# A hybrid decoder layer on one core: an order of emission written with other clock estimates, and a lead of its own for two steps

## The chip, the cores and the metric

The kernel runs on one core of a Trainium2 chip. Its time is the device time of one execution in microseconds (us), and lower is better. The span of a profile is the time from the first to the last instruction that the profiler saw.

The engines go by the profile's names: PE multiplies matrices (PEld loads its weights), ACT applies functions and copies, DVE and POOL work elementwise, SP issues the transfers (DMA). Each engine runs its own queue strictly in the order in which the program emitted it. An instruction that waits for data holds back everything behind it on that engine.

## What is computed

The reference is one decoder layer. A normalised input h (2048 tokens by 1024) is multiplied by a wide matrix w_in; one part of the result feeds a gated delta rule with 8 heads in chunks, the other a short gated convolution; both meet in a second product with w_out.

```python
h = rmsnorm(x, norm_in_w)
proj = h @ w_in
qkv, z_g, b_g, a_g, gate_b, gate_c, h_c, z_c = jnp.split(proj, split_at, axis=-1)
qkv = jax.nn.silu(causal_depthwise_conv(qkv, conv_qkv_w))
...
o = gated_delta_rule_chunked(q, k, v, g, beta)
o = rmsnorm(o, gdn_norm_w) * jax.nn.silu(z_g)
y_c = gate_b * (causal_depthwise_conv(gate_c * h_c, conv_w) + conv_b)
y_c = y_c * jax.nn.silu(z_c)
return rmsnorm(x + jnp.concatenate([o, y_c], -1) @ w_out, final_norm_w)
```

## The kernel before

**The products.** The tokens are taken in two halves of 1024. The columns of w_in are taken in 32 pairs of 128 columns, numbered 0 to 31 here, and each half has one "quad" per pair: seven block products, each of 4 x 3 matmuls of 128x512 in f16 that write the tile ps_d, so 84 matmuls for a quad. They are called large products here. The gates add 40 more behind the quad of pair 0. Counting the large products in PE's queue, the quad of pair p (p from 1 on) begins after 84 p + 40 of them. After both halves come 1536 large products with w_out.

**The preparation of a pair.** In the first half the weights of each pair are made on the way. `fetcher` has SP load two tiles `raw` of 512 KB (four such buffers in all, so a pair's loads wait until an earlier pair is done with). `scales` squares both tiles on ACT, with the sums of the rows in the tile `wss` (written as junk_sq,wss<-raw); one small matmul on PE with a matrix of ones, ps_t<-wss,ones_b, sums them over the partitions. It is called the column sum here. DVE and POOL make a scale `wsc` of it (the tile p on the way); ACT and DVE then write the high and the low f16 part of each weight block (g<-raw), and PE's products read g. SP stores g to DRAM (wc), and the second half only loads it again (gr).

**The order.** The program that emits the instructions keeps a clock of its own for each engine (`Clock`): `cost` is what an instruction is thought to take, `emit` books it and says when its result is thought to be there, transfers included. Steps are generators. `do` emits an instruction once its inputs are thought to be ready by the present time of PE plus a lead (`LEAD`: -0.4 us for PE, 0 for ACT, DVE and POOL, -2.0 for SP); until then other steps and the large products go first. `either` chooses between POOL and DVE for some elementwise steps by the two clocks. At the end `keep_order` fixes each engine's queue in just this order, so these clocks say nothing of how long anything takes on the chip, but they decide what stands behind what.

**The other work.** For each head and half `gdn` prepares the chunks and runs the recurrence (matmuls to ps_r and ps_o, and elementwise steps on DVE and ACT between them); `invert` works through a triangular inverse on POOL (nb, nbt) and goes through DRAM (nd, wd) on the way in and out; `gdn_post` ends a half head (its matmul with `fold` reads the tile op). `later_x` brings in the second half's tokens.

Of the kernel before, what the change touches and what calls it, by code (L numbers as in the profile page):

```python
# [12 lines left out]
BF16 = mybir.dt.bfloat16  # L13
I32 = mybir.dt.int32
AF = mybir.ActivationFunctionType
# [6 lines left out]
DRAM = bass.MemoryType.DRAM  # L22
BACK = 1.2
DRAIN, SEM = 0.2, 0.06
LEAD = {"PE": -0.4, "ACT": 0.0, "DVE": 0.0, "POOL": 0.0, "SP": -2.0}
ORDER = ("PE", "ACT", "DVE", "POOL", "SP")


def is_ap(x):
    return hasattr(x, "tensor") and hasattr(x, "ap")  # L30


class Clock:
# [11 lines left out]
    def box(self, ap):  # L45
        ten = ap.tensor
        name = ten.name
        row = self.rows.get(name)
        if row is None:
            row = 0  # L50
            if ap.space != DRAM:
                row = 1
                for n in list(ten.shape)[1:]:
                    row *= n
            self.rows[name] = row
        pat = list(ap.ap)
        off = ap.offset
        if row:
            p0, f0 = divmod(off, row)
            p1 = p0 + pat[0][1]  # L60
            pat = pat[1:]
        else:
            p0, p1, f0 = 0, 1, off
        f1 = f0 + 1
        for step, n in pat:
            f1 += abs(step) * (n - 1)
        return name, p0, p1, f0, f1

    @staticmethod
    def latest(entries, b, eng):  # L70
# [34 lines left out]
    def cost(self, eng, op, outs, ins, a, k):  # L105
        o = outs[0]
        n = 1
        for s in list(o.shape)[1:]:
            n *= s
        ps = any(x.space == PSUM for x in ins) or o.space == PSUM  # L110
        if eng == "PE":
            if op == "transpose":
                return max(0.06, 0.11 * n / 128)
            lhs = a[1]
            if lhs.dtype == F32:
                return max(0.066, 4 * n / 2370 + 0.006)
            if lhs.dtype == F32R:
                return n / 2370 + 0.013
            return n / 2370
        if eng == "ACT":  # L120
            func = a[2] if len(a) > 2 else k.get("func")
            d = (n + (205 if ps else 246)) / 1200
            if is_ap(k.get("scale")) or is_ap(k.get("bias")):
                d += 0.09
            if "accum_out" in k:
                d += 0.2
            if func in (AF.Exp, AF.Silu):
                if self.func != func:
                    d += 1.29
                self.func = func  # L130
            return d
        if eng == "DVE":
            if op == "tensor_reduce":
                n = 1
                for s in list(ins[0].shape)[1:]:
                    n *= s
            if op in ("tensor_scalar", "tensor_copy", "memset") and not ps:
                return (n / 2 + 110) / 960 + 0.06
            d = (n + 150) / 960 + (0.06 if op == "scalar_tensor_tensor" else 0.0)
            return d if ps or n < 256 else 1.08 * d  # L140
        if eng == "POOL":
            if k.get("op") == ALU.pow:
                return 0.55 + 0.185 * n
            if op == "tensor_tensor":
                return 0.4 + min(0.0028 * n, 0.1 + 0.002 * n)
            return 0.2 + 0.0011 * n
        return 0.4

    def emit(self, eng, op, a, k):
        self.n += 1  # L150
        outs, ins = self.parts(a, k)
        start = max(self.t[eng], self.ready(eng, a, k))
        d = self.cost(eng, op, outs, ins, a, k)
        who = eng
        if eng == "SP":
            who = "DMA"
            self.t[eng] = start + d
            n = 1
            for s in list(outs[0].shape):
                n *= s  # L160
            size = 2 if outs[0].dtype in (F16, BF16) else 4
            self.dma = max(self.dma, start + 1.2) + n * size / 190e3 + 0.1
            done = max(self.dma, start + 1.5 + n * size / 110e3) + 0.8
            free = done
        else:
            self.t[eng] = free = start + d
            done = free + (DRAIN if eng == "PE" else SEM)
        now = self.t["PE"]
        for store, aps, t in ((self.wr, outs, done), (self.rd, ins, free)):
            for ap in aps:  # L170
                b = self.box(ap)
                old = [e for e in store.get(b[0], ()) if e[4] > now - 1.0]
                old.append((b[1], b[2], b[3], b[4], t, who))
                store[b[0]] = old
                if self.last.get(b[0], 0.0) < t:
                    self.last[b[0]] = t
# [36 lines left out]
def hybrid_layer_kernel(ctx, tc, x, norm_in_w, w_in, conv_qkv_w, A_log, dt_bias, gdn_norm_w,  # L213
# [3 lines left out]
    PE, ACT, DVE, POOL, SP = (Engine(clk, r, k) for r, k in zip(  # L217
        (nc.tensor, nc.scalar, nc.vector, nc.gpsimd, nc.sync), ORDER))
# [46 lines left out]
    def const(shape, name, dt=F32):  # L265
        return const_.tile(shape, dt, tag=name, name=name)

    tasks, done = [], set()
    marks, seq = [0], [0]

    def now():
        return clk.t["PE"]
# [6 lines left out]
    def mark(*key):  # L279
        done.add(key)  # L280
        marks[0] += 1
# [35 lines left out]
    def need(*keys):  # L317
        while not all(k in done for k in keys):
            yield None
# [4 lines left out]
    def do(fn, *a, back=BACK, lead=None, **k):  # L324
        e = fn.eng
        lead = LEAD[e] if lead is None else lead
        while True:
            t = clk.ready(e, a, k)
            cur, q = now(), clk.t[e]
            late = t > (cur if lead < 0 else max(cur, q)) + lead  # L330
            if not late and q <= cur + back:
                break
            yield max(t - max(lead, 0.0) if late else 0.0, q - back, cur + 0.1)
        fn(*a, **k)
# [12 lines left out]
    def acq(kind):  # L347
        while not slots[kind]:
            yield None
        return bank(kind)  # L350
# [5 lines left out]
    def rel(x, n=1):  # L356
        if isinstance(x, str):
            cred[x] += n
        else:
            name = x.tensor.name  # L360
            kind, tag = where.pop(name)
            where[tag] = clk.last.get(name, 0.0)
            slots[kind].append(tag)
        marks[0] += 1
# [47 lines left out]
    for half in range(2):  # L412
        convs = [(f, half, g) for g in range(G) for f in ("ca", "cb")]
        for i in range(H):
# [3 lines left out]
            n = ((4, 2, 2, 2, 2, 2, 1, 1), (2, 1, 2, 1, 2, 1, 2, 2))[half][i]  # L418
# [42 lines left out]
    ones_b = const([P, P], "ones_b", BF16)  # L461
# [26 lines left out]
    def pow2_below(o, sq, gain):  # L488
        n = sq.shape[-1]
        r = sm.tile([P, 2], F32, tag="p2", name="p2")[:, 0:n]  # L490
        yield from do(DVE.tensor_scalar, r, sq, 1e-30, None, op0=ALU.max)
        yield from do(POOL.tensor_tensor, r, r, nhalf_pow[:, 0:n], op=ALU.pow)
        yield from do(DVE.tensor_tensor, r.bitcast(I32), r.bitcast(I32), expo[:, 0:n].bitcast(I32),
                      op=ALU.bitwise_and)
        yield from do(DVE.tensor_scalar, o, r, gain, None, op0=ALU.mult)
# [199 lines left out]
    def scales():  # L695
        for p in range(NP):
            yield from need(("raw", p))
            s2, inv1, rho = (wsc[:, p, j:j + 1] for j in (1, 2, 4))
            ss = sm.tile([P, 2], F32, tag="wss", name="wss")
            for j in range(2):  # L700
                yield from do(ACT.activation, junk_sq, raws[p, j].rearrange("p k c -> p (k c)"),
                              AF.Square, accum_out=ss[:, j:j + 1])
            pt = yield from acq("t")
            yield from do(PE.matmul, pt[:, 0:2], ones_b, ss.bitcast(BF16)[:, 1::2], start=True, stop=True)
            yield from pow2_below(wsc[:, p, 0:2], pt[:, 0:2], 8192.0)
            rel(pt)
            yield from do(DVE.reciprocal, wsc[:, p, 2:4], wsc[:, p, 0:2])
            yield from do(DVE.tensor_scalar, rho, s2, inv1, None, op0=ALU.mult)
            yield from do(DVE.tensor_scalar, wsc[:, p, 2:4], wsc[:, p, 2:4], isx, None, op0=ALU.mult)
            mark("s", p)  # L710
# [787 lines left out]
    spawn(fetcher(), 0)  # L1498
    first_x()
    spawn(scales(), 0)  # L1500
    spawn(prepare_hi(), 1)
    spawn(prepare_lo(), 1)
# [105 lines left out]
```

## Time and profile before

| | |
|---|---|
| time, median of 3 runs | 2168.21 us (2161.38 to 2171.83) |
| the profiled execution's own time | 2169.81 us |
| its span | 2168.1 us |
| mean granted TensorE clock | 0.945 |
| busy: PE, DVE, POOL, ACT | 1940.2, 1391.7, 977.0, 968.1 us |
| moved by DMA | 302.66 MB, 139 GB/s over the span |

The table says that PE is the busiest engine, with 228 us of the span in which it runs nothing. To see where, one reads the 40 slices of the page first (each 54 us wide), then the busy time by stretches, and in a stretch with gaps the list of instructions in order of time with the idle time before each and what ended it. The granted clock has two levels, 1.0 (2.4 GHz) and 0.5 (1.2 GHz); a mean between them tells how much of a stretch ran at either.

### The profile page before, as it was taken

How to read it: one execution, taken by the hardware profiler on the slowest of the kernel's cores; microseconds unless marked ns; L12 is line 12 of the kernel's file. 1: busy time of each engine (PE TensorE's matmuls, PEld its weight loads, DVE VectorE, ACT ScalarE, POOL GpSimd, SP SyncE). 2: the span in 40 equal slices, each digit the busy share in tenths (PEclk: the TensorE clock that was granted, in tenths of full speed). 3: DMA queues.
4: the chain of work that ended last, by engine and by line, in shares of the span. 5: the costliest groups of instructions: out<-in, count | busy, mean ns of one | idle time of the engine just before them, and what ended most of it. 6: DMA issues, size and time to landing. Idle time of an engine off the chain costs nothing.

```text
span 2168.1 us, 29898 instructions
## 1 busy us (share of the span) xinstructions
PE 1940.2 (89%) x10832; PEld 1058.4 (49%) x10832; DVE 1391.7 (64%) x2547; ACT 968.1 (45%) x1889; POOL 977.0 (45%) x1228
## 2 busy tenths in 40 slices
PE   3699885889687979898999999999999999999998
PEld 2244342435444545454455655555655655444443
DVE  5689865886677877886466667766767644433221
ACT  6465555455353554644254444453543423333210
POOL 2226721286556736475366538467457451100000
PEclk9899987999798989998999999999999999999999
DMA  6348666355474765557354445545543447343210
GB/s 172 82 106 200 164 172 162 102 134 148 69 145 69 174 120 147 121 140 265 108 170 153 156 130 185 187 141 187 179 123 112 127 130 296 112 141 107 69 49 29
DMA packets 231194, 302.66 MB, mean 140 GB/s; under 512 B 48381, under 2 KB 161414, under 8 KB 230150
## 3 DMA queue, kind: packets, MB, share of 16 engines
q1 hardware_dynamic: 231046, 300.75, 50.3%
q8 instruction: 85, 1.39, 0.3%
q14 instruction: 63, 0.52, 0.1%
HBM read 188.36 MB, written 112.33 MB: 139 GB/s over the span
## 4 chain that ended last, share of the span: by engine, by line
PE 53%; DVE 2%; issue 1%; ACT 1%; DMA 1%; POOL 0%; DVEq 0%; POOLq 0%; SPq 0%; ACTq 0%
PE ps_d L188 44%; PE ps_t L188 5%; PE ps_r L188 3%; PE ps_o L188 2%; DVE kq L188 1%; DMA raw<-in_w_in_dram 1%; DVE c L188 0%; ACT c L188 0%; ACT junk_sq L188 0%; ACT L188 0%; DVE vacc L188 0%; DVE p L188 0%; DVE zb L188 0%; ACT sq L188 0%; DVE wq L188 0%
## 5 line engine op out<-in xcount | busy, mean ns | idle before, releaser
L188 PE MATMUL ps_d<-xop,g 128*128 128x512 f16 x2688 | 660.9, 397 | 37.2 <-ACT xop L188 12.8
L188 PE MATMUL ps_d<-xop,gr 128*128 128x512 f16 x2688 | 651.1, 382 | 0.0
L188 PEld LDWEIGHTS <-g 128*128 128x128 f16 x2688 | 269.1, 102 | 383.7 <-issue 115.0
L188 POOL TENSOR_TENSOR nbt<-nb 32x30 f32<-32x30 f32 (+14 forms) x480 | 320.7, 668 | 148.6 <-DMA nb<-nd 114.1
L188 PEld LDWEIGHTS <-gr 128*128 128x128 f16 x2688 | 261.8, 99 | 242.2 <-issue 6.3
L188 ACT ACTIVATE c<-ps_d 128x512 f32<-128x512 f32 x320 | 189.9, 594 | 374.4 <-PE ps_d L188 365.9
L188 POOL TENSOR_TENSOR nb<-nb,nbt 32x30 f32<-32x30 f32 (+14 forms) x480 | 323.7, 674 | 35.5
L188 PE MATMUL ps_d<-wo,mm 128*128 128x512 f16 x1536 | 336.7, 381 | 3.2 <-ACT mm L188 3.2
L188 PEld LDWEIGHTS <-mm 128*128 128x128 f16 x1536 | 149.7, 98 | 184.8 <-ACT mm L188 5.1
L188 POOL TENSOR_TENSOR oss<-oss,nhalf_pow 128x16 f32<-128x16 f32 x32 | 96.1, 3002 | 166.5 <-DVE oss L188 148.3
L188 DVE SCALAR_TENSOR_TENSOR kq<-c,wq,kq 128x512 f32<-128x512 f32 x192 | 164.4, 862 | 8.1 <-ACT kq L188 3.9
L188 POOL TENSOR_TENSOR p<-p,nhalf_pow 128x2 f32<-128x2 f32 (+1 forms) x51 | 40.2, 788 | 283.3 <-DVE p L188 275.2
L188 DVE SCALAR_TENSOR_TENSOR res<-ps_d,msc,res 128x512 f32<-128x512 f32 x32 | 22.6, 747 | 193.8 <-PE ps_d L188 193.8
L188 DVE SCALAR_TENSOR_TENSOR g<-raw,wsc,g 128x1024 f16<-128x1024 f32 (+1 forms) x96 | 114.2, 1194 | 8.9 <-ACT g L188 8.5
L188 ACT ACTIVATE g<-raw,wsc 128x1024 f16<-128x1024 f32 (+1 forms) x96 | 95.7, 1002 | 50.3 <-PE ps_d L188 32.1
L188 DVE TENSOR_TENSOR c<-ps_d,c 128x512 f32<-128x512 f32 x128 | 87.5, 684 | 44.5 <-PE ps_d L188 44.0
L188 ACT ACTIVATE junk_sq<-raw 128x1024 bf16<-128x1024 f32 x64 | 67.5, 1055 | 96.0 <-DMA raw<-in_w_in_dram 95.0
L188 POOL TENSOR_TENSOR stat<-stat,nhalf_pow 128x1 f32<-128x1 f32 x16 | 9.1, 570 | 217.7 <-DVE stat L188 216.8
L188 DVE TENSOR_TENSOR c<-c,c 128x1024 f32<-128x1024 f32 (+1 forms) x70 | 71.3, 1019 | 46.6 <-ACT c L188 43.9
L188 ACT ACTIVATE mm<-mr,msc 128x1024 f16<-128x1024 f32 x32 | 36.0, 1148 | 138.6 <-PE ps_d L188 111.6
L188 POOL TENSOR_TENSOR c<-c,c 128x512 f32<-128x512 f32 (+1 forms) x26 | 42.7, 1642 | 121.3 <-ACT c L188 87.9
L188 ACT ACTIVATE u<-ps_r 128x128 f32<-128x128 f32 x128 | 35.1, 274 | 124.7 <-PE ps_r L188 124.0
(226 smaller groups left out, 2793.1 us busy)
## 6 DMA issues: line engine op xcount, KB each, us to landing
gr<-wc SPq DMA_DIRECT2D x96, 512.0 KB, 3.8
raw<-in_w_in_dram SPq DMA_DIRECT2D x64, 512.0 KB, 10.3
wc<-g SPq DMA_DIRECT2D x64, 512.0 KB, 8.6
wc<-g SPq DMA_DIRECT2D x96, 256.0 KB, 2.7
wor<-in_w_out_dram SPq DMA_DIRECT2D x32, 512.0 KB, 5.4
mr<-mixd SPq DMA_DIRECT2D x32, 512.0 KB, 5.3
x<-in_x_dram SPq DMA_DIRECT2D x16, 512.0 KB, 6.7
E<-gd SPq DMA_DIRECT2D x16, 512.0 KB, 5.4
```

The source lines that it names most:

```text
L188: return raw(*a, **k)
```

## The change

Three things change, all of them in the program that emits.

The clock prices a transfer otherwise. Before, all transfers shared 190 KB per us with 0.1 us each, began 1.2 us after the issue and counted as landed 0.8 us after their end, with 110 KB per us as the most for a single one. Now the rate depends on the shorter contiguous run of the two sides (330 KB per us x run / (run + 700), run in bytes, by the new function `run_of`), the start is 1.5 us after the issue and the landing 2.5 us after the end. A tile of `raw` has runs of 512 bytes.

POOL's two-operand steps are priced at 0.3 us + 0.0023 us per element, where it was 0.4 us + the lesser of 0.0028 and 0.1 + 0.002 per element.

The squares of a pair from 1 on get a lead of -4.0 us (`SAFE`), and their column sum one of -3.0 us, in place of 0 and -0.4.

```diff
+SAFE = -4.0
...
+    def run_of(ap):
+        run, rest = 1, list(ap.ap)
+        if ap.space != DRAM:
+            rest = rest[1:]
+        for step, n in reversed(rest):
+            if step == run:
+                run *= n
+            elif n > 1:
+                break
+        return run
...
             if op == "tensor_tensor":
-                return 0.4 + min(0.0028 * n, 0.1 + 0.002 * n)
+                return 0.3 + 0.0023 * n
...
-            self.dma = max(self.dma, start + 1.2) + n * size / 190e3 + 0.1
-            done = max(self.dma, start + 1.5 + n * size / 110e3) + 0.8
+            run = min(self.run_of(outs[0]), self.run_of(ins[0])) * size
+            self.dma = max(self.dma, start + 1.5) + n * size / (330e3 * run / (run + 700)) + 0.1
+            done = self.dma + 2.5
...
                 yield from do(ACT.activation, junk_sq, raws[p, j].rearrange("p k c -> p (k c)"),
-                              AF.Square, accum_out=ss[:, j:j + 1])
+                              AF.Square, accum_out=ss[:, j:j + 1], lead=SAFE if p else None)
             pt = yield from acq("t")
-            yield from do(PE.matmul, pt[:, 0:2], ones_b, ss.bitcast(BF16)[:, 1::2], start=True, stop=True)
+            yield from do(PE.matmul, pt[:, 0:2], ones_b, ss.bitcast(BF16)[:, 1::2], start=True, stop=True,
+                          lead=-3.0 if p else None)
```

Every engine's queue comes out in another order, from the first 100 us to the last head. Three places follow, each before and then changed. Numbers behind names only tell one buffer from another; they differ between the two programs.

The first is PE's queue at the column sum of pair 13. Before, it stands behind the same large product as pair 12's (the first row), ahead of the quad of pair 11:

```order
L188 MATMUL ps_t_2882<-wss_2764,ones_b_168 128x2
L188 MATMUL ps_t_2920<-ident_161,x2_620 128x128 x2
L188 MATMUL ps_t_2920<-ident_161,x2_621 128x128 x2
L188 MATMUL ps_t_2938<-ident_161,x2_620 128x128 x2
L188 MATMUL ps_t_2938<-ident_161,x2_621 128x128 x2
L188 LDWEIGHTS ones_b_168
L188 MATMUL ps_t_2949<-wss_2915,ones_b_168 128x2
L188 MATMUL ps_r_2983<-S_all_214,kq_849 128x128
L188 MATMUL ps_o_2982<-kq_849,S_all_214 128x128
L188 MATMUL ps_r_2983<-r_2984,Wt0_215 128x128
L188 MATMUL ps_t_2995<-ident_161,kq_2966 128x128
```

Changed (the first row is a large product of the quad of pair 11):

```order
L202 MATMUL ps_d_3119<-xop_226,g_2916 128x512
L202 MATMUL ps_t_3180<-kq_2979 128x256 x2
L202 LDWEIGHTS ones_b_168
L202 MATMUL ps_t_3154<-wss_2974,ones_b_168 128x2
L202 MATMUL ps_r_3139<-u_3191,kst_1250 128x128
L202 MATMUL ps_o_2963<-NA_1296,u_3191 128x128
L202 LDWEIGHTS g_2916
```

It stood behind 964 large products and stands behind 1033, inside the quad of pair 11 instead of ahead of it.

The second is ACT's queue at the squares of pair 19 (kss are sums for the keys of a head, c1 and c2 results of the quads, u and oc belong to the recurrence). Before:

```order
L188 ACTIVATE kq_4378<-c2_3728,wq_3889 128x4x128
L188 ACTIVATE c2_4169<-c2_4169,wsc_123 128x1024
L188 ACTIVATE u_4446<-ps_r_4419 128x128
L188 ACTIVATE junk_sq_156,wss_4430<-raw_4404 128x1024
L188 ACTIVATE junk_sq_156,wss_4430<-raw_4363 128x1024
L188 ACTIVATE junk_4464,kss_4381<-ps_t_4423 128x128
```

Changed:

```order
L202 ACTIVATE junk_4629,kss_4290<-ps_t_4571 128x128
L202 ACTIVATE c2_4552<-ps_d_4616 128x512
L202 ACTIVATE junk_sq_156,wss_4525<-raw_4510 128x1024
L202 ACTIVATE junk_sq_156,wss_4525<-raw_4474 128x1024
L202 ACTIVATE oc_4671<-ps_o_4301 128x512
L202 ACTIVATE g_4660<-st_4489,wsc_123 128x512
```

The sums for the keys, which stood behind the squares, stand ahead of them now, and so does a result of the quad. PE's column sum of this pair went from behind 1468 large products to behind 1536.

The third is PE's queue where the quad of pair 8 begins. Before (g_2141 is the first weight block of pair 8; the column sum of that pair stands 28 large products ahead of it, outside this piece):

```order
L188 LDWEIGHTS g_2059
L188 MATMUL ps_d_1996<-xop_224,g_2059 128x512
L188 LDWEIGHTS g_2141
L188 MATMUL ps_d_2191<-xop_221,g_2141 128x512
L188 LDWEIGHTS g_2141
```

Changed (g_2351 is that block there):

```order
L202 MATMUL ps_r_2314<-S_all_214,kq_732 128x128
L202 LDWEIGHTS ones_b_168
L202 MATMUL ps_t_2276<-wss_2000,ones_b_168 128x2
L202 LDWEIGHTS g_2196
L202 MATMUL ps_d_2044<-xop_224,g_2196 128x512
L202 LDWEIGHTS g_2196
L202 MATMUL ps_d_2044<-xop_224,g_2196 128x512
L202 MATMUL ps_o_2219<-kq_732,S_all_214 128x128
L202 MATMUL ps_r_2314<-r_2315,Wt0_215 128x128
L202 MATMUL ps_r_2314<-u_2335,kst_1124 128x128
L202 MATMUL ps_o_2219<-NA_1184,u_2335 128x128
L202 MATMUL ps_r_2344<-S_all_214,kq_732 128x128
```

Between this column sum and the quad that needs it stand two large products and a step of the recurrence now.

Over all 32 pairs the column sum stands later in 28, by 3 to 96 large products, at the same place in 2 and earlier in 2. `either` sends ten steps to POOL that went to DVE.

## Rows read from the trace of the kernel before

**Rows 1.** The page: busy time by engine; the 40 slices of PE and its clock.

```profile
PE 1940.2 (89%) x10832; PEld 1058.4 (49%) x10832; DVE 1391.7 (64%) x2547; ACT 968.1 (45%) x1889; POOL 977.0 (45%) x1228
PE   3699885889687979898999999999999999999998
PEclk9899987999798989998999999999999999999999
```

**Rows 2.** Busy time by stretches: span, length, engines (instructions), PE clock, DMA share, GB/s.

```profile
100.00:1050.00 950.00, 793.76 (x4328) 432.06 (x4327) 712.36 (x1268) 494.32 (x941) 499.12 (x577) 0.90 0.59 143
400.00:1000.00 600.00, 508.03 (x2847) 283.37 (x2846) 468.11 (x800) 302.90 (x577) 371.19 (x444) 0.90 0.57 130
1050.00:1800.00 750.00, 743.27 (x4648) 436.70 (x4647) 497.49 (x906) 319.06 (x680) 421.25 (x573) 0.99 0.48 150
1800.00:2168.00 368.00, 352.60 (x1652) 163.35 (x1650) 115.93 (x243) 96.55 (x168) 26.28 (x34) 0.99 0.33 113
```

**Rows 3.** The tile wss: its matmuls, and PE's idle us before them (times).

```profile
L188 PE MATMUL ps_t<-wss,ones_b x32: 163/163/167, 29.7 to 957.5; 128*128 128x2 bf16 x32
...
  ACT junk_sq L188: 74.3, 17
```

**Rows 4.** PE in order of time: start, us, instruction, idle before it and its end.

```profile
360.65 0.16 PE L188 MATMUL ps_t<-wss,ones_b 128*128 128x2 bf16 x1 [1.16 <-ACT junk_sq L188]
...
373.57 0.16 PE L188 MATMUL ps_t<-wss,ones_b 128*128 128x2 bf16 x1 [11.51 <-ACT junk_sq L188]
...
569.03 0.16 PE L188 MATMUL ps_t<-wss,ones_b 128*128 128x2 bf16 x1 [10.94 <-ACT junk_sq L188]
...
624.39 0.16 PE L188 MATMUL ps_t<-wss,ones_b 128*128 128x2 bf16 x1 [9.59 <-ACT junk_sq L188]
...
688.76 0.16 PE L188 MATMUL ps_t<-wss,ones_b 128*128 128x2 bf16 x1 [8.93 <-ACT junk_sq L188]
...
780.84 0.16 PE L188 MATMUL ps_t<-wss,ones_b 128*128 128x2 bf16 x1 [7.53 <-ACT junk_sq L188]
```

**Rows 5.** The wait of 10.94 us: second load's issue, ACT's square, five us within.

```profile
547.91 0.38 SPq L188 DMA_DIRECT2D raw<-in_w_in_dram  x1
...
566.64 1.06 ACT L188 ACTIVATE junk_sq<-raw 128x1024 bf16<-128x1024 f32 x1 [13.23 <-DMA raw<-in_w_in_dram]
...
560.00:565.00 5.00, 0.00 (x0) 0.00 (x0) 0.00 (x0) 0.00 (x0) 0.00 (x0) 0.50 0.79 91
```

**Rows 6.** Stretches at half clock behind nine such waits: two of them, and the sum.

```profile
569.00:575.20 6.20, 6.17 (x19) 3.45 (x19) 3.15 (x12) 1.70 (x10) 5.03 (x11) 0.50 0.01 3
...
780.80:797.00 16.20, 11.78 (x39) 7.47 (x39) 15.23 (x31) 9.77 (x26) 5.16 (x3) 0.50 0.56 111
...
sum 61.50, PE 51.64 PEld 27.26 DVE 47.91 ACT 37.44 POOL 29.65; mean PE 5.74 PEld 3.03 DVE 5.32 ACT 4.16 POOL 3.29
```

**Rows 7.** The tile raw: time from issue to landing.

```profile
DMA to landing us min/median/max: 5.8/10.3/20.2
```

**Rows 8.** PE between the column sum of pair 8 and its quad.

```profile
255.29 0.17 PE L188 MATMUL ps_t<-wss,ones_b 128*128 128x2 bf16 x1
255.32 6.20 PE L188 MATMUL ps_d<-xop,g 128*128 128x512 f16 x28
262.25 0.60 PE L188 MATMUL ps_d<-xop,g 128*128 128x512 f16 x2 [0.73 <-ACT g L188]
```

**Rows 9.** PE's wait for DVE at 447 us, and the 20 us ahead of it.

```profile
446.77 0.61 PE L188 MATMUL ps_t<-op,fold 128*128 128x16 f32 x2 [9.88 <-DVE op L188]
...
425.00:445.00 20.00, 11.90 (x62) 6.04 (x59) 17.86 (x23) 10.87 (x27) 18.75 (x25) 0.93 0.41 120
```

**Rows 10.** Groups by form, POOL and DVE; then one DVE instruction in order of time.

```profile
L188 DVE TENSOR_TENSOR c<-c,c 128x1024 f32<-128x1024 f32 x25 | 33.3, 1331 | 4.2 <-ACT c L188 3.6
...
L188 POOL TENSOR_TENSOR c<-c,c 128x1024 f32<-128x1024 f32 x7 | 17.1, 2450 | 44.0 <-ACT c L188 21.4 <-PE ps_t L188 20.6 <-DVE c L188 2.0
...
258.50 2.30 DVE L188 TENSOR_TENSOR p<-p,expo 128x2 int32<-128x2 int32 x1
```

More of the change, by code (lines that the diff above doesn't have):

```diff
@@ L67, in box @@
         return name, p0, p1, f0, f1
+    @staticmethod
+    def run_of(ap):
[8 more added lines that the diff above has]
+        return run
     @staticmethod
```

## The prediction

> **What bounds the kernel now.** I read the page's busy times and slices first. PE runs 1940 of 2168 us, and the slices show where it does not: from about the twenty-first on it stands at nine tenths and full clock, ahead of that it has gaps, and its clock falls in the same slices [rows 1]. The busy times by stretches say it in us. From 1050 us to the end PE is idle for 22 us only, so there is next to nothing to win: that part is bounded by PE's own work. From 100 to 1050 us it is idle for 156 us, with a mean clock of 0.90 [rows 2]. No other engine is full there: DVE, the next, is busy for 712 of the 950 us.
>
> I then asked what PE's idle time ends with. One cause stands out: the column sums of the weight pairs, 74.3 us in 17 waits for ACT's square [rows 3]. In order of time six of them are the waits ahead of pairs 12, 13, 19, 20, 22 and 25 (a column sum belongs to one pair, in this order, 32 in all) [rows 4]. What PE waits for through ACT is a transfer: at pair 19 the second load was issued at 547.9 us, ACT took up the square at 566.6 after 13.2 us of nothing, and PE got on at 569.0. For five us in between every engine shows 0.00 [rows 5]. That is not an engine at work; both queues have stopped at an instruction that was emitted too early, and all others ran dry behind them. A load takes 10.3 us from issue to landing in the median and 20.2 at most [rows 7]. The code before counted 1.5 + 524/110 + 0.8 = 7.1 us for one alone.
>
> **The change part by part.** *The later squares and column sums.* The first three of the 17 waits lie ahead of 60 us and come to about 2.8 us, so some 71.5 us are in reach. How far each moves is read from the two orders, and what that is worth from 28 large products in 6.20 us, 0.22 us each [rows 8]. Pair 13 moves by 69 large products, 15.2 us against a wait of 11.5; pair 19 by 68, 15.0 against 10.9; pair 20 by 48, 10.6 against 9.6. These are covered. Pair 22 moves by 28, 6.2 against 8.9, which leaves 2.7; pair 25 by 6 only, 1.3 against 7.5, which leaves 6.2 (a block of the recurrence that stood behind it went elsewhere, so nothing else covers it for certain); pair 12 stays, with its 1.2 us. The shorter waits (pairs 3, 14, 18, 27, 29, 31 and others) move by 14 to 50, more than their length. Left are 10.1 us; recovered 71.5 - 10 = 61 us. The first bound is 71.5, if pairs 22 and 25 are also covered by work on the way.
>
> *The clock behind the waits.* Behind nine of them PE ran at 0.5 of its clock, busy for 51.6 us in all [rows 6]. At full clock that would have been half, 25.8 us. In proportion to the waits that go (61 of 71.5), I take 22 us; 0 to 26 are the ends.
>
> *What the later column sum costs.* It is the head of a chain: scale, high part, low part, first product. At pair 8 the chain took 262.25 - 255.29 = 7.0 us, and the 28 large products between covered 6.2 of it [rows 8]. From pair 12 on 39 to 106 large products stand between column sum and quad in the new order, 8.6 us or more, so the cover holds. For pairs 5, 6, 7, 8, 9 and 11 only 30, 18, 28, 2, 24 and 24 are left. At 7.0 us less 0.22 us each that is 0.4 + 3.0 + 0.8 + 6.5 + 1.7 + 1.7 = 14 us if no other PE work stands between, and 0 if the recurrence fills it; at pair 8 a step of it does stand there. I take 10, nearer to the sum, since the orders show little else at pairs 6 and 9.
>
> *What comes late next.* DVE was idle in the empty stretches too, and its work doesn't get less. From 400 to 1000 us it is busy for 468 of 600 us [rows 2]; without some 65 us of stops that is 468/535 = 87%. Where it is near full already, PE waits for it: 17.9 busy us of the 20 ahead of 445, then 9.9 us of PE behind the tile op [rows 9]. I book one more such wait, 10 us; the ends are 0 and 30 (three, one for each stretch in which DVE has a backlog today).
>
> *Prices of transfers and of POOL.* These move everything else: steps that read what was transferred come later, steps behind the inverse sooner. In the second half PE is full, so a new order there has 22 us to win at most; against it stands nothing that the trace shows, and I take 0, with 10 us either way. Ten steps go from DVE to POOL, five of them of 128x1024, where one takes 2.45 us instead of 1.33 [rows 10]. Neither engine's own queue bounds the kernel, so I book nothing. What POOL's longer use costs DVE shows in one row: an instruction on 128x2 numbers took 2.30 us at 258.5 [rows 10]. The Trainium skill says why that may be (GPSIMD Engine Reference, section "Key points"): GpSimd shares its SBUF interfaces with VectorE and contends with instructions that read two SBUF inputs. By that rule the ten steps would hold DVE up by at most their own length, an estimate of 10 x 2.45 = 25 us from the row, and if all of that reached PE the time would be 2130 instead of 2105; the trace shows such long DVE instructions, but not that PE waited for them as a rule.
>
> The sum: 61 + 22 - 10 - 10 = 63 us. The profiled execution's own time is 2169.8 us (span 2168.1), so 2107; it stands 1.6 us above the median of the runs, so **2105 us**. The ends of the parts: at most 71.5 + 26 + 10 = 107 us gained (2061), at least 61 - 14 - 30 - 10 = 7 (2161). They hardly all fall on one side, so the forecast itself reaches from 2080 to 2140.
>
> **The rivals.** *Nearly all comes back.* The chain has more cover than large products alone, DVE's work spreads into the stops that are gone, and small waits of the same kind go with them. Then 71.5 + 26 and a little more: about 2065 (2045 to 2080). For it speaks that all engines were empty in the stops; against it DVE at 87%.
>
> *PE stops at the next thing.* Pairs 13, 19 and 25 waited at the edge of a quad, where recurrence steps stand in a row. If PE then only waits for those, the 30 us of the three and 11 of the clock stay: 63 - 41 = 22 us, 2146 (2140 to 2158). Against it: at pair 19 PE went on with recurrence and quad at once when the stop ended.
>
> *Nothing.* The estimate of a transfer isn't its time; the orders move by the former. If landings come later by as much, because loads are issued later in SP's new queue, the waits stay: 2158 to 2179. The orders say that 28 of 32 column sums did move, so the change does what it says; what speaks for this is only the wide spread of landings [rows 7].
>
> *Slower.* The chain from column sum to product becomes the bound. Ten pairs (4 to 11, 26, 28) have 42 large products or fewer between, 287 in all, some 62 us of cover. With a chain of L the price is 10 L - 62. A chain held up in DVE as the tile op was has 7 + 9.9 = 17 us, so 108 us, 25 more than the 83 that are won: 2193 (2180 to 2210). It decides from L = 14.5 us on. Against it: 7.0 us in the row that shows it plainly, and cover by recurrence steps.
>
> **How the numbers follow.** Forecast 2105: 0.55. Nearly all back: 0.17. Next thing: 0.10. Nothing: 0.08. Slower: 0.10. About 0.5%, 11 us, is what a measurement here tells from no change; so faster by more has 0.55 + 0.17 + 0.10 = 0.82, no difference 0.08, slower 0.10. The range of 8 in 10 holds the forecast, most of "nearly all" and the "next thing": 2055 to 2160; the forecast's own is 2080 to 2140.
>
> **What would show it.** Right: PE's waits for junk_sq ahead of wss fall from 74 to some 10 us, the largest at pairs 22 and 25; half-clock time from 100 to 1050 us shrinks with them; the stretch from 1050 us on keeps its length within 10 us; waits for g grow by some 10 us between 170 and 340 us. Wrong: waits for junk_sq stay above 40 us; waits for g or for DVE's tiles grow by more than 40; or the second half changes by more than 10 us.

## The result, and the profile after

The changed kernel takes **2099.82 us** (median of 4 runs, 2094.53 to 2100.22), against 2170.02 for the kernel before on the same chip (2161.38 to 2172.77): a ratio of 0.968 with a 95% interval of 0.965 to 0.971, so 70 us less. The forecast was 2105, in a range from 2055 to 2160.

The profiled execution of the changed kernel is its fastest, 2094.53 us with a span of 2092.8. It is 75.3 us shorter than that of the kernel before, and its readings below make up those 75.3.

From the page of the changed kernel, its busy times and two rows of its 40 slices, which answer to [rows 1]:

```profile
PE 1914.5 (91%) x10832; PEld 1041.8 (50%) x10832; DVE 1390.3 (66%) x2547; ACT 960.5 (46%) x1879; POOL 1003.3 (48%) x1238
...
PE   3798996798888989888999999999999999999998
...
PEclk9899998899898999999999999999999999999999
```

PE issues the same 10,832 matmuls and is busy for 25.7 us less. As the work is the same, that is put down to the clock: seven slices of the last row were below 9, and five are. The rest of the 75.3, 49.6 us, is idle time (2168.1 - 1940.2 = 227.9 before, 2092.8 - 1914.5 = 178.3 now).

Busy time by stretches in the changed kernel (the columns are those of [rows 2]); the last two rows divide the span at large product 2728, the end of the first half's quads:

```profile
100.00:1050.00 950.00, 833.15 (x4715) 450.48 (x4713) 756.83 (x1361) 518.88 (x1008) 551.65 (x629) 0.94 0.62 151
400.00:1000.00 600.00, 524.02 (x3076) 290.79 (x3074) 476.78 (x820) 312.10 (x605) 419.72 (x490) 0.95 0.62 147
1050.00:1800.00 750.00, 743.57 (x4574) 434.87 (x4573) 476.29 (x862) 305.41 (x640) 406.38 (x540) 1.00 0.51 162
...
100.00:965.70 865.70, 754.70 (x4220) 405.33 (x4218) 701.85 (x1245) 481.98 (x923) 504.58 (x568) 0.94 0.62 145
965.70:2092.80 1127.10, 1107.65 (x6402) 609.41 (x6400) 619.76 (x1163) 416.96 (x851) 469.45 (x628) 1.00 0.45 146
```

The same cut in the kernel before:

```profile
100.00:1006.20 906.20, 759.04 (x4086) 409.47 (x4085) 693.29 (x1226) 479.30 (x908) 488.32 (x556) 0.90 0.59 139
1006.20:2168.10 1161.90, 1130.60 (x6540) 622.65 (x6538) 632.49 (x1189) 430.63 (x882) 458.33 (x628) 0.99 0.44 141
```

Read the first number, the length, then PE's busy time and its instructions in brackets. Up to product 2728 the changed kernel is 40.5 us shorter: 36.2 us less idle (147.2 and 111.0), and 4.3 us less busy although 134 more matmuls stand there. From there on it is 34.8 us shorter: 11.8 less idle, and 23.0 less busy with 138 fewer matmuls and a clock of 1.00 for 0.99.

The tile wss of the changed kernel, for [rows 3]:

```profile
L202 PE MATMUL ps_t<-wss,ones_b x32: 163/167/211, 28.0 to 910.7; 128*128 128x2 bf16 x32
...
  ACT junk_sq L202: 9.7, 3
```

What PE waits for in the whole of the changed kernel (us in total, times, the longest; here junk_sq counts other small matmuls too, hence 11.1):

```profile
PE ps_d L202 <- ACT c L202: 26.0, 9, 6.0
PE ps_r L202 <- DVE r L202: 15.0, 13, 3.5
PE ps_r L202 <- DVE S_all L202: 14.4, 11, 2.8
PE ps_t L202 <- DVE vp L202: 11.7, 1, 11.7
PE ps_d L202 <- ACT xop L202: 11.3, 4, 6.3
PE ps_t L202 <- ACT junk_sq L202: 11.1, 4, 7.6
```

And the same view's row for c in the kernel before:

```profile
PE ps_d L188 <- ACT c L188: 4.7, 3, 3.1
```

So 64.6 us went from under one name, and some 21 us came under another, c, the copy of a large product out of PSUM. One of these waits is the old one. PE and ACT of the changed kernel at pair 22, in order of time:

```profile
639.70 6.21 PE L202 MATMUL ps_d<-xop,g 128*128 128x512 f16 x28
651.63 1.01 PE L202 MATMUL ps_d<-xop,g 128*128 128x512 f16 x2 [5.72 <-ACT c L202]
...
640.76 0.60 ACT L202 ACTIVATE c<-ps_d 128x512 f32<-128x512 f32 x1 [0.66 <-PE ps_d L202]
648.76 1.06 ACT L202 ACTIVATE junk_sq<-raw 128x1024 bf16<-128x1024 f32 x1 [7.40 <-DMA raw<-in_w_in_dram]
...
649.94 1.06 ACT L202 ACTIVATE junk_sq<-raw 128x1024 bf16<-128x1024 f32 x1
...
651.00 1.06 ACT L202 ACTIVATE c<-ps_d 128x512 f32<-128x512 f32 x2
```

ACT stops for 7.40 us at the square, which waits for its load. The copy c stands behind it in ACT's queue, and PE, behind its 28 products, waits for c. It is the old wait, met at another instruction of PE, and the name at PE doesn't tell. That holds for this wait and not for all of the 21 us: where no square waits for a load (e10 below), c still stands for 19.8 us. The measure that does tell is ACT's own idle time ahead of the squares, put down to the loads. In the kernel before:

```profile
  DMA raw<-in_w_in_dram: 95.0, 19
```

In the changed kernel:

```profile
  DMA raw<-in_w_in_dram: 20.2, 4
```

The reverse occurs too. The longest wait that still bears the square's name in the changed kernel, at pair 12:

```profile
335.76 0.21 PE L202 MATMUL ps_t<-wss,ones_b 128*128 128x2 bf16 x1
...
349.27 0.16 PE L202 MATMUL ps_t<-wss,ones_b 128*128 128x2 bf16 x1 [7.62 <-ACT junk_sq L202]
...
344.01 1.33 ACT L202 ACTIVATE g<-st,wsc 128x512 f16<-128x512 f32 x2 [1.48 <-DVE st L202]
345.25 1.75 ACT L202 ACTIVATE g<-raw,wsc 128x1024 f16<-128x1024 f32 x2
346.90 1.04 ACT L202 ACTIVATE junk_sq<-raw 128x1024 bf16<-128x1024 f32 x1
...
348.07 1.06 ACT L202 ACTIVATE junk_sq<-raw 128x1024 bf16<-128x1024 f32 x1
```

Here no load is late. The column sum of pair 11 (first row), later than before, leads over its scale to the weight blocks g, ACT works through these until 347 (after a wait of 1.48 us for DVE), and pair 12's square stands behind them. By the order of the rows this is the chain that the prediction priced, reaching PE through ACT's queue; e10 shows that no load has a part in it.

### The profile page after: what moved, and what is told of

Same layout as the page of the kernel before. It is cut to its first block, busy times and chain, and to the rows that moved or that the text cites. A ratio compares the mean times of both kernels' runs of the same rounds, so it can differ in the third digit from the quotient of the medians.

```text
span 2092.8 us, 29911 instructions
## 1 busy us (share of the span) xinstructions
PE 1914.5 (91%) x10832; PEld 1041.8 (50%) x10832; DVE 1390.3 (66%) x2547; ACT 960.5 (46%) x1879; POOL 1003.3 (48%) x1238
## 3 DMA queue, kind: packets, MB, share of 16 engines
q8 instruction: 85, 1.39, 0.3%
## 4 chain that ended last, share of the span: by engine, by line
PE 53%; POOL 6%; DMA 4%; DVE 3%; issue 2%; ACT 1%; SPq 0%; DVEq 0%; POOLq 0%; ACTq 0%
PE ps_d L202 43%; PE ps_t L202 6%; POOL nb L202 3%; PE ps_r L202 3%; POOL nbt L202 2%; PE ps_o L202 2%; DMA raw<-in_w_in_dram 1%; DVE kq L202 1%; DVE g L202 1%; DMA wd<-nb 1%; DMA zb<-zd 1%; DMA wc<-g 1%; DVE c L202 0%; DMA mr<-mixd 0%; POOL raw L202 0%
## 5 line engine op out<-in xcount | busy, mean ns | idle before, releaser
L202 POOL TENSOR_TENSOR nb<-nb,nbt 32x30 f32<-32x30 f32 (+14 forms) x480 | 331.5, 691 | 35.8
L202 POOL TENSOR_TENSOR c<-c,c 128x512 f32<-128x512 f32 (+1 forms) x33 | 57.3, 1738 | 159.8 <-ACT c L202 114.8
L202 DVE SCALAR_TENSOR_TENSOR g<-raw,wsc,g 128x1024 f16<-128x1024 f32 (+1 forms) x96 | 116.5, 1221 | 11.5 <-ACT g L202 11.2
L202 ACT ACTIVATE u<-ps_r 128x128 f32<-128x128 f32 x128 | 35.2, 275 | 147.2 <-PE ps_r L202 144.5
L202 POOL TENSOR_TENSOR raw<-raw 128x512 f32<-128x512 f32 x31 | 41.8, 1349 | 119.6 <-DVE st L202 74.4
L202 DVE TENSOR_TENSOR c<-c,c 128x512 f32<-128x512 f32 (+1 forms) x63 | 58.3, 926 | 52.1 <-ACT c L202 49.8
## 6 DMA issues: line engine op xcount, KB each, us to landing
raw<-in_w_in_dram SPq DMA_DIRECT2D x64, 512.0 KB, 11.2
```

The costliest lines, as they stand in the source:

```text
L202: return raw(*a, **k)
```

## The experiments

Theory A is the prediction's: the squares waited for their loads at the head of ACT's queue, and the time went as the squares and column sums moved behind other work. Against it stand that the stops only move on to the next thing (B), that the prices bring the gain by what else they move (C), that one lead alone does it all, and, for larger leads, that the chain from column sum to weight blocks takes over.

The results in one table. "Later" is how many large products later than in the kernel before a column sum stands, as a mean of the 32. "Loads" is ACT's idle time ahead of the squares that ended with a load, read as in the last rows above (with constants in place of the loads there is none); "g" is PE's waits for weight blocks; "2728" is when that large product started, and "rest" what the span has behind it. All but the first three columns and "later" come from one profiled execution, which can be up to 12 us off the median. The kernel before took 2164 to 2170 us in the median beside the different kernels; the ratios are to the runs on the same chip.

| kernel | us (range) | ratio to before, 95% | later | loads, us | g, us | 2728 at | rest |
|---|---|---|---|---|---|---|---|
| before | 2170.02 (2161.38 to 2172.77) | 1 | 0 | 95.0 | 16.0 | 1006.2 | 1161.9 |
| after | 2099.82 (2094.53 to 2100.22) | 0.965 to 0.971 | 27 | 20.2 | 12.6 | 965.7 | 1127.1 |
| e8 before, constant squares | 2109.24 (2105.81 to 2111.22) | 0.972 to 0.977 | 0 | none | 16.3 | 948.4 | 1159.7 |
| e10 after, constant squares | 2099.10 (2098.17 to 2102.03) | 0.966 to 0.971 | 27 | none | 11.2 | 977.1 | 1123.2 |
| e1 leads only | 2127.54 (2123.16 to 2129.07) | 0.981 to 0.985 | 18 | 50.5 | 13.6 | 987.7 | 1137.7 |
| e2 prices only | 2118.96 (2118.44 to 2120.22) | 0.977 to 0.982 | 8 | 64.5 | 9.5 | 966.3 | 1150.4 |
| e3 transfer price only | 2130.31 (2129.45 to 2131.09) | 0.980 to 0.986 | 6 | 60.7 | 8.4 | 985.7 | 1143.5 |
| e4 POOL price only | 2183.13 (2177.82 to 2186.53) | 1.005 to 1.009 | 1 | 116.0 | 14.0 | 1040.4 | 1144.4 |
| e9 without the POOL price | 2106.92 (2097.94 to 2108.78) | 0.968 to 0.974 | 21 | 20.7 | 15.3 | 956.8 | 1139.4 |
| e11 without PE's lead | 2113.60 (2107.45 to 2117.13) | 0.973 to 0.978 | 21 | 31.6 | 17.4 | 966.7 | 1139.0 |
| e12 squares' lead -2 | 2125.42 (2123.22 to 2137.05) | 0.978 to 0.985 | 26 | 39.4 | 17.7 | 979.0 | 1156.3 |
| e6 squares' lead -8 | 2126.89 (2125.03 to 2135.47) | 0.978 to 0.986 | 40 | 6.8 | 33.7 | 976.7 | 1147.7 |
| e7 squares' lead -16 | 2167.86 (2164.93 to 2170.11) | 0.998 to 1.001 | 74 | 1.0 | 100.2 | 1032.2 | 1133.5 |

**The cause alone: e8 and e10.** Both keep an order row for row, and let the squares from pair 1 on read a constant tile in place of the loaded weights (so the scales are not those of the weights); the planner's clock books the old instruction.

```diff
+    def booked(*a, **k):
+        clk.emit("ACT", "activation", a, k)
+        return nc.scalar.activation(junk_sq.rearrange("p (k c) -> p k c", c=P),
+                                    ones.unsqueeze(1).to_broadcast([P, KD, P]), AF.Square,
+                                    accum_out=k["accum_out"])
...
-                yield from do(ACT.activation, junk_sq, raws[p, j]...
+                yield from do(booked if p else ACT.activation, junk_sq, raws[p, j]...
```

e8, in the order before:

> The kernel before with its order of emission unchanged row for row; from pair 1 on the squares read a constant tile of ones in place of the pair's weights (so the scales are other numbers), and no longer wait for the transfer. Theory A (what PE lost were stops at instructions emitted ahead of their data, and the half clock behind them): PE's idle time that ends with the square falls from 74 us to 5 or less, and the time to 2085 to 2115 us. Theory B (the stops only move on: PE waits for the next thing, recurrence or weights): the idle time moves to waits for g or for the recurrence, and the time stays at 2145 to 2175 us.

Measured: 2109, where the kernel before took 2164 beside it. In the order before, this one wait is worth 55 us, with no instruction moved. They lie where A puts them: product 2728 starts 57.8 us earlier, and the rest is as long as before (1159.7, 1161.9). Theory B has a small part: PE's waits for r, a tile of the recurrence, grew, first before, then in e8.

```profile
PE ps_r L188 <- DVE r L188: 8.5, 11, 1.4
...
PE ps_r L188 <- DVE r L188: 20.1, 15, 8.4
```

The residue is larger than expected. PE's waits ahead of the column sums in e8:

```profile
  ACT junk_sq L697: 13.0, 5
```

No load is behind these 13.0, only ACT's queue: the longest, 8.0 us, is at pair 13, where ACT works through a weight block and the tiles o and xa, some of which DVE releases one by one. In the kernel before, the wait at pair 13 is the longest of [rows 4], 11.51 us, and ACT stopped there for its load for only 3.42: the larger part of it was never the load's. So of the 74.3 us some 61 were the loads' [rows 3].

e10, in the changed order:

> The changed kernel's order, row for row, with the squares from pair 1 on reading a constant tile of ones instead of the loaded weights (so the scales are not those of the weights; the work per instruction is the same). If the 9.7 us of waits for junk_sq that are left in the changed kernel are the last that the loads cost PE through the squares: they fall to 3 us or less and the time to 2085 to 2097 us. If ACT itself is late there (its queue stops at other things), waits and time stay within 5 us of the changed kernel's.

Measured: 2099.10 against 2099.82, no difference. The wait at pair 12 stays at 7.47 us with no load to wait for:

```profile
350.36 0.16 PE L202 MATMUL ps_t<-wss,ones_b 128*128 128x2 bf16 x1 [7.47 <-ACT junk_sq L711]
```

So it is ACT's queue, as read above. The wait for c at pair 22 is gone in e10, but PE stops there all the same; c's total, then PE and DVE of e10 in order of time:

```profile
PE ps_d L202 <- ACT c L202: 19.8, 7, 6.0
...
653.87 2.08 PE L202 MATMUL ps_t<-kq 128*128 128x256 f32 x4 [6.43 <-DVE kst L202]
...
651.28 0.43 DVE L202 STREAM_TRANSPOSE Vt<-Wt 32x256 f32<-32x256 f32 x1 [7.12 <-DMA Wt<-wd]
```

DVE stands at a transpose that waits for a transfer of its own, the inverse on its way back from DRAM, and kst, which PE needs, stands behind it. The changed kernel has this stop of DVE too, for 7.77 us beside ACT's 7.40. At pair 19 it has another: ACT stops for 7.56 us for the load, DVE for 6.88 at the transpose, and PE for 5.99; in e10 5.81 of PE's are left. Over the whole kernel DVE's stops at this transpose come to 8.9 us before and 17.1 now. It is the pattern of the squares on another engine: at these two pairs PE would stop without the late loads too, so they cost nothing that can be told.

Together e8 and e10 divide the 70 us. With the loads' wait taken away the two orders differ by 0.6% (0.975 and 0.968 of the kernel before, and the intervals don't meet), some 13 us. So some 55 of the 70 are the loads', and the others are what else the new order moves.

**The edits one by one: e1 to e4.** e1 is the kernel before with the two leads; the prices are old.

```diff
+SAFE = -4.0
...
-                              AF.Square, accum_out=ss[:, j:j + 1])
+                              AF.Square, accum_out=ss[:, j:j + 1], lead=SAFE if p else None)
...
-            yield from do(PE.matmul, pt[:, 0:2], ones_b, ..., start=True, stop=True)
+            yield from do(PE.matmul, pt[:, 0:2], ones_b, ..., start=True, stop=True,
+                          lead=-3.0 if p else None)
```

> The kernel before with the two leads alone (-4.0 and -3.0), both prices as before. The column sums stand 18 large products later on the mean (27 with the whole change). Theory A: PE's waits for the square fall to 10 to 25 us and the time to 2105 to 2135 us. Theory C (the gain came from the prices, which move recurrence and transfers): 2150 to 2175 us.

e2 is the changed kernel without the leads (the same lines taken back), and with a line that keeps the start's steps in order, which its other order needs; e3 and e11 have it too:

```diff
+                yield from need(("x", X11, kt), ("x", X21, kt))
```

> The changed kernel without the two leads: both prices new. (A need is added in the start so that one step is not emitted ahead of the step whose result it reads.) The column sums stand 8 large products later on the mean, pairs 12, 13 and 25 not at all. Theory A: waits for the square 35 to 60 us, time 2130 to 2160 us. Theory C: 2095 to 2115 us, with the waits still there.

e3 and e4 are the kernel before with one price each:

```diff
-            self.dma = max(self.dma, start + 1.2) + n * size / 190e3 + 0.1
-            done = max(self.dma, start + 1.5 + n * size / 110e3) + 0.8
+            run = min(self.run_of(outs[0]), self.run_of(ins[0])) * size
+            self.dma = max(self.dma, start + 1.5) + n * size / (330e3 * run / (run + 700)) + 0.1
+            done = self.dma + 2.5
```

> The kernel before with the new price of transfers alone (and the added need in the start). The column sums stand 6 large products later on the mean, pairs 12, 13, 17, 22 to 25 hardly or not. Theory A: waits for the square stay at 45 to 70 us, time 2140 to 2170 us. Theory C (prices): 2100 to 2120 us.

```diff
-                return 0.4 + min(0.0028 * n, 0.1 + 0.002 * n)
+                return 0.3 + 0.0023 * n
```

> The kernel before with the new price of POOL's steps alone. The column sums stand 1 large product later on the mean. Theory A: waits for the square as before, 60 to 85 us, time 2160 to 2180 us. Theory C: below 2140 us.

Measured, by the ratios: in e1 the leads bring 37 us; in e2 the prices 44; in e3 that of the transfers alone 38; in e4 that of POOL costs 15. Leads and prices together bring 70, not 81. That is not because both take from the same waits: ACT's waits for loads fall by 44.5 us with the leads, by 30.5 with the prices and by 74.8 with both. By the profiled executions what doesn't add up lies ahead of product 2728, which starts 18.5, 39.9 and 40.5 us earlier; its cause stays open. The prices alone bring more than A gave them, and e2 and e3 lie between the ranges of A and C, so C is partly right. The prices move the column sums by 8 products only, yet they take 30 us of ACT's waits for loads and shorten the rest by 11.5 us.

e4 tells most on how to read. At PE the squares' name stands for less than before, while ACT waits more for the loads. PE's first two waits in e4:

```profile
PE ps_t L201 <- ACT junk_sq L201: 55.1, 14, 12.8
PE ps_d L201 <- ACT c L201: 33.2, 10, 12.4
```

ACT's idle time ahead of its squares in e4:

```profile
  DMA raw<-in_w_in_dram: 116.0, 19
```

By PE's row for the squares (75.5 us in this view of the kernel before) the kernel should have gained 20 us; by ACT's row it should have lost, as it did.

**Which lead, and how much: e5, e11, e12, e6, e7.** e5 and e11 take PE's lead away and keep the squares'.

```diff
-            yield from do(PE.matmul, pt[:, 0:2], ones_b, ..., start=True, stop=True,
-                          lead=-3.0 if p else None)
+            yield from do(PE.matmul, pt[:, 0:2], ones_b, ..., start=True, stop=True)
```

> The changed kernel without the column sum's lead on PE; the square's lead on ACT stays. The column sums stand 20 large products later on the mean. Theory A with the transfer as what is late: the square's lead does nearly all, so waits for the square under 20 us and 2100 to 2115 us. If the 3 us on PE were needed of themselves (PE meets a square that has only just begun): waits of 2 to 3 us at some twenty pairs, 40 to 60 us in all, and 2130 to 2155 us.

In e5's order one step of the start stands ahead of the step whose result it reads; it took 2110.98 us. e11 is the same with these steps in order:

> The changed kernel without PE's own lead for the column sum (the squares' lead of -4.0 us and both prices stay), with the start steps in their right order. Column sums stand 21 large products later than before. If the squares' lead does the work (a column sum that is emitted after them follows them anyhow): waits for junk_sq at 20 us or less, 2098 to 2108 us. If PE's lead has its own part, as the run with the start steps the other way round had it (37 us of waits, 2111 us): 30 to 45 us of waits, 2108 to 2120 us.

Measured: 2114, with these first waits of PE:

```profile
PE ps_t L202 <- ACT junk_sq L202: 41.2, 9, 7.5
PE ps_d L202 <- ACT c L202: 22.1, 6, 12.4
```

So PE's own lead has a part. Ahead of the column sums alone PE waits for 39.7 us in e11: 21.1 are at pairs 19, 20, 22 and 25, whose squares ACT begins 4.5 to 8.4 us late for a load, and 18.6 at pairs 2, 11, 12 and 29, where no load is late and ACT comes to the square late.

The other three change the squares' lead.

```diff
-SAFE = -4.0
+SAFE = -2.0
```

> The changed kernel with a lead of -2.0 us for the squares instead of -4.0. Column sums stand 26 large products later than before, against 27. Leads of -8 and -16 gave 27 and 68 us back. If the loss to a late chain begins at -4 already, less lead is faster: 2080 to 2095 us. If at -4 it is nothing and the waits come back below: waits for junk_sq 15 to 35 us, 2100 to 2115 us. In between, 2095 to 2100, the lead has a flat best here.

> The changed kernel with the square's lead at -8.0 in place of -4.0. The column sums stand 40 large products later on the mean than before the change (27 with it); at pairs 6 and 10 they stand right ahead of the quad that needs them. Theory A: the waits for the square that are left (10 us) go, some 5 to 10 us of waits for g come: 2090 to 2110 us. If the chain from column sum to product were the bound already: 2120 us or more.

> The changed kernel with the square's lead at -16.0. The column sums stand 74 large products later on the mean than before the change; 26 of the pairs have 0 to 26 large products left ahead of their quad. The chain as the prediction priced it (7.0 us less 0.22 us for each large product between) gives 114 us of waits for g against 14 with the change: 2180 to 2210 us. If recurrence steps cover the chain instead: 2095 to 2130 us.

Measured: 2125 at -2, 2100 at -4, 2127 at -8, 2168 at -16. In the table the waits for loads fall all the way (39.4, 20.2, 6.8, 1.0) while those for g grow behind -4 (12.6, 33.7, 100.2). In e7 the chain is what bounds the first half:

```profile
PE ps_d L202 <- ACT g L202: 61.2, 23, 12.1
PE ps_d L202 <- DVE g L202: 39.0, 29, 3.6
```

That is the rival "slower" in kind, with 100 us of waits where 114 were expected for e7. (The 108 of the prediction were for a longer chain, 17 us, in the changed kernel's order, so they are no measure here.) The kernel comes out even with the one before, not behind it, since the rest stays 28 us shorter. At -2 and -8 not all is the squares' or the chain's: against the changed kernel 13 and 11 us are lost up to product 2728, and 29 and 21 behind it, where no square stands. What lengthened that part stays open, and e12 came out above every range that was expected for it.

**Without POOL's price: e9.**

> The leads and the new price of transfers, with POOL priced as before. Column sums stand 21 large products later than before on average (27 with all three edits, 18 with the leads alone). If the squares' place decides (theory A): waits for junk_sq stay at 10 to 20 us, and the time is 2100 to 2115 us. If each price has an effect of its own that adds up (POOL's price alone cost 15 us), the kernel is faster without it: 2080 to 2092 us.

Measured: 2106.92, 7 us above the changed kernel, with intervals that touch (0.968 to 0.974, 0.965 to 0.971). The price that costs 15 us alone costs nothing that can be told beside the others; effects of such edits don't add up. PE's waits ahead of the column sums, 3.5 us, came out below the range. No kernel of the study beats the changed one.

## Why the prediction was right, point by point

**The cause holds.** The 17 waits were the loads', for some 61 us of 74.3: e8 shows it with the order untouched, and e10 that in the changed order nothing of it is left that can be told. The longest of the six waits that the prediction names, at pair 13, was read wrongly: most of it was ACT's own queue. Over the kernels of the table the time follows ACT's waits for loads only loosely: the ends agree (116.0 and 95.0 us for 2183 and 2170, 31.6 to 20.2 for 2114 to 2100), and between them it doesn't (64.5, 60.7, 50.5 and 39.4 us for 2119, 2130, 2128 and 2125). "Nothing" falls: the loads did land later, 11.2 us in the median instead of 10.3 [rows 7], and the squares waited less all the same.

**Waits recovered, 61 of 71.5.** In name 74.3 - 9.7 = 64.6. What was in reach is 73.5: of the 17 only one, of 0.77 us, lies ahead of 60 us, and the two others that were counted there (2.0 us) end with the tile xf. The column sums of pairs 13, 19 and 20 have no wait, as read from the orders. That of pair 25 fell from 7.53 to 1.65, where 6.2 was to stay; ACT's stop for its load fell from 10.48 to 3.36 there. For pair 22, 2.7 us were to stay, and 5.72 did, under c. Pair 12 was to keep 1.2 [rows 4] and has 7.62, from ACT's queue. "PE stops at the next thing" came at pair 19, with the 5.99 us above, and not at 13 and 25.

**The clock, 22.** Too much for the place it was booked for. Up to product 2728 PE is 4.3 us less busy, with some 9 us of work moved in (below), so about 13 came there (the clock's records, 114 and 77 us busy at 0.5, would make it 18); as much again came in the second half. The proportion was sound. In e8 the instructions are the same, and up to product 2728 its row reads:

```profile
100.00:948.40 848.40, 743.62 (x4090) 400.97 (x4090) 695.88 (x1226) 478.85 (x909) 493.35 (x556) 0.93 0.64 149
```

Against the kernel before PE's busy time fell by 15.4 us there beside 42.4 us less idle time, 0.36 us for each (22 of 61 is 0.36). What was wrong is to take it of the waits that go, 61, and not of the idle time that goes, 36.

**The later column sum, 10.** Near in size by luck, and in the wrong place. PE's waits for g between 170 and 340 us did not grow by 10 but fell from 14.7 to 9.8. Product 712 starts 8.7 us later, but not for waits: from 100 us to there PE has 818 matmuls in place of 668, 154.8 us of work in place of 145.3, and idles no more than before. The chain itself cost its 7.62 us once, at pair 12. What was missed is that a chain held up need not show at PE's next product; it can stop ACT, and with it the next pair's square.

**DVE late next, 10.** One such long wait came, and the one that was there went. PE, then DVE in the 12 us ahead of it:

```profile
420.35 1.08 PE L202 MATMUL ps_t<-ident,vacc 128*128 128x128 f32 x4 [11.74 <-DVE vp L202]
...
408.52 1.08 DVE L202 SCALAR_TENSOR_TENSOR st<-raw,wsc 128x512 f32<-128x512 f32 x1 [4.20 <-POOL raw L202]
409.64 2.18 DVE L202 TENSOR_TENSOR raw<-raw,st 128x512 f32<-128x512 f32 x1
411.74 2.09 DVE L202 TENSOR_TENSOR kq<-qe,kq 128x512 f32<-128x512 f32 x2
```

The wait for op of 9.88 us [rows 9] is gone (it stands in e8 as before, at 10.0, so it is the order that removes it). These two make 2 us. Over all of DVE's tiles PE's waits rose by 5, from 77 to 82 us: those for r and S_all, tiles of the recurrence, by 10.3 (8.5 to 15.0 and 10.6 to 14.4), while the others together fell. So about half of the 10 came, in small pieces. Not booked were ACT's: waits for c rose by 21 us, of which some 6 are a load's (26.0, and 19.8 in e10). DVE starts its backlog here because it waited 4.20 us for POOL, and its second instruction takes 2.18 us where the five of its kind take 0.97 in the median. POOL was busy for 18.9 of the 20 us from 400 on. That agrees with what the Trainium skill says (GPSIMD Engine Reference, "Key points"): GpSimd (POOL here) shares its SBUF interfaces with VectorE (DVE), and VectorE instructions with two SBUF inputs contend with it. The 25 us that were bounded by that rule did not come: e9, without POOL's price, is no faster.

**The second half, 0 within 10.** This step failed, and with it one of the prediction's own signs of being wrong came: from product 2728 on the changed kernel is 34.8 us shorter. In that stretch idle time alone, 22 us from 1050 on, was taken for all that a new order could win, and nothing of it was booked. From product 2728 on 11.8 us of idle time did go, and 27 of 31 us at half clock, by the records of the clock (up to 14 us of PE's time), which the prediction did not count there. It also left out the 138 small matmuls, the remaining 9 us or so of the 23.0, which moved to the first half, where PE had stops to put them in. e8, which moves nothing, gains 2.2 us there; each of the kernels with another order gains 6 to 39.

Put together, the prediction booked 41 us of idle time (61 - 20) and 22 of clock for the first half and nothing for the second. What came was 36 and about 13 in the first, 12 and up to 14 in the second, which makes 75 for the profiled execution and 70 by the medians. By place, 63 us were booked for the first half and 40.5 came; nothing was booked for the second and 34.8 came. The cause was right; that the sum lies so near is in good part luck, one step too high beside one too low.

## What to carry to other kernels

Where all engines show nothing at once, look for the instruction at the head of an in-order queue that was emitted ahead of its data, and measure the idle time of the engine that stops at the transfer, not of the one that suffers: here the names at PE said 55 us where ACT's said 116. Then look at the other engines for the same pattern: here ACT's stops went, and DVE's at its transposes grew. Such an instruction can also stand too late, since the chain that hangs on it is delayed with it (at -16 it cost 100 us of waits and the whole gain). Of the leads tried -4 is the best (2125, 2100, 2127 and 2168 us at -2, -4, -8 and -16), but two thirds of what -2 and -8 lose lie where no square stands. Edits to a planner's prices don't add up, and each reorders everything, so a shift of some 20 us between two such versions can lie far from what the edit is about.

## What the runs showed of the hardware that was not expected

A short stop of PE can be followed by a stretch at half clock of several times its length. In the second half of e12, PE in order of time:

```profile
1222.78 1.80 PE L202 MATMUL ps_t<-kq 128*128 128x256 f32 x4 [1.39 <-DVE NA L202]
```

And the busy times of the stretch that follows:

```profile
1223.00:1233.20 10.20, 10.20 (x52) 5.85 (x52) 3.02 (x9) 2.85 (x12) 0.40 (x1) 0.50 0.61 182
```

After 0.7 us of products of 32x32 and 1.39 us of nothing, with PE busy before and behind, the granted clock is 0.50 for 10.2 us; by an estimate from this row that is 5.1 us lost behind 1.39. It needn't be so: a stop of 1.87 us in the same trace is followed by full clock.

```profile
1447.80 0.66 PE L202 MATMUL ps_t<-ident,vacc 128*128 128x128 f32 x4 [1.87 <-ACT vacc L202]
...
1447.70:1459.70 12.00, 11.88 (x58) 5.76 (x58) 5.65 (x5) 5.25 (x10) 11.14 (x16) 1.00 0.43 139
```

In the changed kernel PE has no stop to speak of from 1180 to 1700 us, and its clock there is 1.00:

```profile
1180.00:1700.00 520.00, 519.91 (x3327) 307.79 (x3326) 350.27 (x622) 217.71 (x466) 313.05 (x414) 1.00 0.49 153
```

e12's profiled execution was its slowest, 12 us above its median, so what such stops cost it as a rule stays open.
